# Two more up-projection chunks by seven products, four sums of down weights moved, and two copies put behind the norms, in a two-layer decoder trunk

## The chip, the cores and the metric

One core of one Trainium2 chip runs the whole program. The metric is the device time of one execution in microseconds (us); lower is better. The engines are named as in the profile: PE is TensorE (PEld its weight loads), DVE is VectorE, ACT is ScalarE, POOL is GpSimd and SP is SyncE, which here only issues DMAs.

## The reference, cut to what matters

```python
D_MODEL = 1024; SEQ = 512; DEPTH = 2; D_FF = 2816; CONV_W = 3

def conv_ffn(xn, w_up, cw, cb, w_down):
    a = xn @ w_up                                   # (512, 1024) x (1024, 5632)
    ap = jnp.pad(a, ((0, 0), (CONV_W - 1, 0), (0, 0)))
    a = sum(ap[:, j:j + T] * cw[j] for j in range(CONV_W)) + cb
    gate, val = jnp.split(a, 2, axis=-1)
    return (jax.nn.gelu(gate, approximate=True) * val) @ w_down

def reference(...):
    h = x
    for l in range(DEPTH):
        if l == 0: mix = dilated_mixer(rms_norm(h, g[0]), w_qkv_a[0], w_o_a[0], cos, sin)
        else:      # keys, values and forget gates are projected once from h
            kvf = rms_norm(h, kv_norm) @ w_kvf
            mix = fox_mixer(rms_norm(h, g[0]), w_q_b[0], w_o_b[0], k_sh, v_sh, c_sh)
        h = h + rms_norm(mix, g[1])
        h = h + rms_norm(conv_ffn(rms_norm(h, g[2]), w_up[l], conv_w[l], conv_b[l], w_down[l]), g[3])
    return h
```

All inputs are float32.

## The kernel before, in words

**Precision.** Each large product is made of three: an operand is split into a high part (a copy to the type fp32r, on ACT) and a low part (what is left, by a subtraction on DVE, or by a DMA that adds on the way, issued by POOL), and `mm3` adds high x high, high x low and low x high in PSUM. Its three lines are L292 to L294. In two forms `mm3` runs with a moving operand 512 wide or 256 wide.

**Weights.** `Weights` (`W`) hands out the weights in a fixed list of pieces of 128 x 1024. `load` issues the DMA on SP two pieces ahead, `high` makes the copy (L60) and `low` the subtraction (L69); `high_added` is a copy, a negated copy (L62) and the adding DMA (L86). `W.get()` returns the next piece and splits those up to `W.ahead` - 1 further, so the highs and lows of later pieces enter the queues of ACT and DVE at the place of that call. The order on each engine is the order in which the program is written.

**One layer.** Attention, output projection, up-projections in 22 chunks (a chunk is 128 columns of the gate and 128 of the value), down-projection. `h` stays on chip.

*The output projection* (`Proj.finish`) first takes two 128-row chunks of the weight through all four blocks of 128 positions, and then the last four chunks block by block, so that the blocks end one after the other. In the first layer a function `late` is called half-way through the first part. After each half block `Boundary.half` runs: mean square, multiply by the gain (`mix`, L337), the residual (L344), and, delayed by one block, the next norm (`norm`: square on ACT at L299, multiply on DVE at L309), and, delayed by two, `transpose`: eight PE transposes (L360), the split into `xh` and `xl` (L363, L364), and for blocks 0 and 1 two copies of the transposed values into `xlow` on ACT (L464); for blocks 2 and 3 two differences on DVE (L468, L469). `first_products` then begins chunks 0 and 1 with the first half of the positions, before blocks 2 and 3 are transposed.

*The up-projections* (`ffn`). A plain chunk multiplies two pieces with all 512 positions: 2 x 8 x 3 matmuls 512 wide. A chunk in `SEVEN` takes the product of 2 x 2 blocks by seven products of blocks instead of eight; each is 4 x 3 matmuls 256 wide:

```python
prod(o2, w.pop("S2"), (*XB, HI)); prod(o3, w.pop("S3"), (*XA, HI), True)
prod(o1, w.pop("A12"), x21);      prod(o2, w.pop("S1"), (*XA, LO))
prod(o3, w.pop("A22"), (*XB, LO));  opened = open_seven(m)   # A11 of the next chunk
prod(o2, w.pop("S4"), x22)
```

Between them stand three additions in PSUM on DVE (L1043, L1047, L1048) and copies on ACT (`u2` L1033, `s7` L1038, `s1` L1004). The weights of a seven-product chunk are made from two raw pieces in eight steps by the generator `seven_weights` (L732 to L764), advanced by `step` for the next chunk `m` and the one after, `n`. Each chunk's result passes the convolution taps (ACT L670, twice DVE L674), the GELU (L698), the product of gate and value on POOL (`product`, L693) and a DMA to `hD`. `post` does the taps and the GELU of a plain chunk one chunk later.

*The down-projection* works on pairs of 128-row chunks of the weight, 11 pairs, also by seven products. For it each pair needs four sums of weight blocks. `down_sums` makes these: three loads on SP, four subtractions on DVE (L639 to L642), and two stores of 512 KB to `dT`, from where `W` later loads them as pieces. It is a generator that its caller advances with `next`; `lag` and `behind` say how many calls later the subtractions and the stores follow the load. In this kernel the 22 pairs are summed so: ten of layer 0 and two of layer 1 beside the first projections, (0, 10) and (1, 8) in chunks 19 and 20 of layer 0, (1, 0) and (1, 1) beside the keys, four of layer 1 in the second attention, (1, 10) and (1, 9) in chunks 19 and 20 of layer 1. The activations of a pair are read back (`pair_load`), summed (`pair_sums`, L809 to L811), and their high and low parts are made by `pair_highs` (L819) and `pair_lows` (L824) for the first pairs while the last chunks still run.

**Memory.** Tiles come from pools of fixed slots: `t8` has 16 of 8 KB a partition, `t4` ten of 4 KB, `t2` eight of 2 KB, and PSUM has eight banks. An instruction that needs a slot waits until its last user is done.

Of the kernel before, what the change touches and what calls it, by code (L numbers as in the profile page):

```python
# [24 lines left out]
BIG = 3.0e38  # L25


SEVEN = tuple(range(3, 19))
ND = NF // 2
WARM = 6, 3  # L30
HALVES = [(slice(0, 1024),), (slice(0, 512), slice(512, 1024))]
# [77 lines left out]
def trunk_kernel(ctx, tc, x, norm_gains, w_qkv_a, w_o_a, w_q_b, w_o_b, kv_norm, w_kvf, b_f,  # L109
# [11 lines left out]
    def t8(shape, dt=F32, name="t8"):  # L121
        return p8.tile(shape, dt, tag="t8", name=name)
# [306 lines left out]
    class Boundary:  # L429
# [5 lines left out]

        def __init__(self, gain_mix, gain_next, name):
            self.mix, self.gain_next, self.name = Mix(gain_mix), gain_next, name
            self.xn, self.r = {}, {}
            self.xT = None

        def half(self, i, n, hf, o):
            b = self.order[i]
            self.mix.half(b, n, hf, o)
            if n == 0:
                if i >= 2:
                    self.transpose(self.order[i - 2])
                if i >= 1:
                    self.norm(self.order[i - 1])
            else:
                self.mix.add(b)  # L450

# [4 lines left out]
        def transpose(self, b):  # L456
            if self.xT is None:
                self.xT = new_xT(self.name)
                self.low = t8([128, 2, 4, 256], name="xlow")
            pts = transpose_in(b, self.xn.pop(b), self.xT)  # L460
            s = slice(b % 2 * 128, b % 2 * 128 + 128)
            if b < 2:
                for i, pt in enumerate(pts):
                    act.copy(self.low[:, i, :, s], pt)  # L464
# [127 lines left out]
    def first_products(bd, n):  # L592
        bd.norm(3)
        outs = [bank([128, T], name="first") for _ in range(n)]
        ws = []
        for i, o in enumerate(outs):
            ws.append(W.get())
            feat_mm(ws[i], bd.xT, o, LO)
            if i == 0:
                bd.transpose(2)  # L600
            if i == 2:
                bd.transpose(3)
        for w, o in zip(ws, outs):
            feat_mm(w, bd.xT, o, HI)
        return outs
# [58 lines left out]
    def ffn(l, bd, cp, nxt, ahead):  # L664
# [32 lines left out]
        def glu(c, bb):  # L697
            act.activation(bb[:, 0, :], bb[:, 0, :], AF.Gelu_apprx_tanh)  # L698
            gated.append((c, bb))

        def post(c, banks, between=None, bb=None):
            product()
            if bb is None:
                bb = taps(c, banks, between)
            else:
                first_tap(bb, 0, banks[0], c)
                other_taps(bb, 0, banks[0], c)
            glu(c, bb)

        xT = None  # L710
# [53 lines left out]
            dve.tensor_tensor(v[:, 1], r0, v[:, 0].bitcast(F32), ALU.subtract)  # L764

        def plain_weights(c):
            for _ in range(2):
                if c < NF - 2:
                    W.high_added()
                else:  # L770
                    W.high()
                    yield
                    W.low()
                if c < NF - 2:
                    yield

        gens = {}

# [6 lines left out]
            for _ in range(n):  # L785
                next(gens[c], None)

        def prepare(c, part):

            n = c + 2  # L790
            if n < NF and n not in SEVEN:
                step(n, 2 if part == 0 and n < NF - 2 else 1)
# [5 lines left out]
        def pair_load(j):  # L798

            if j < ND:  # L800
                acts[j] = k = t8([128, 1024], name="dact")
                sp.dma_start(k[:, 0:512], hD[2 * j])
                sp.dma_start(k[:, s2_], hD[2 * j + 1, :, 256:512])

# [184 lines left out]
        step(S0, 2)  # L989
        post(0, first[0:2])  # L990
        step(S0, 2)
        post(1, first[2:4])
        del first
        begun = opened = half_taps = None
        before = None

        def prod(o, w, x, start=False):
            half_mm(o, w, x[0:2], x[2], start)
# [8 lines left out]
        for c in range(2, NF):  # L1007
            if c == NF - 4:
                pair_load(0)
            if c == NF - 3:  # L1010
                sums = down_sums([(l, ND - 1), (1, 8 + l)], in_one, [pool], 1, 0)
                next(sums)
            m, n = c + 1, c + 2
            if c in SEVEN:
                x21, x22 = [(xT[0][i], xT[1][i], s) for i, s in ((1, LO), (1, HI))]
# [37 lines left out]
                if m in SEVEN:  # L1053
                    opened = open_seven(m)
                    step(m)
                else:
                    begun = W.get(), bank([128, T], name="up")
                    up(*begun, range(4))
                    step(n)
                other_taps(half_taps, 1, banks[1], NF + c)  # L1060
                prod(o2, w.pop("S4"), x22)
            else:
                banks = [bank([128, T], name="up") for _ in range(2)]
                for s in range(2):
                    if s == 0 and begun:
                        w, banks[0] = begun
                        up(*begun, range(4, KD))
                        begun = None
                    else:
                        up(W.get(), banks[s], range(KD))  # L1070
                    if c == NF - 2:
                        next(sums)
                    if s == 0 and before:
                        post(*before, (lambda: pair_lows(0)) if c == NF - 1 else None, half_taps)
                        half_taps = None
                        if c >= NF - 2:
                            pair_highs(c - NF + 2)
                            pair_sums(c - NF + 3)
                    if s == 0:
                        prepare(c, 0)  # L1080
                        if m in SEVEN:
                            opened = open_seven(m)
                    prepare(c, 1 + s)
                    if n in SEVEN:
                        step(n, 2)
            before = c, banks
            if c == NF - 3:
# [365 lines left out]
    combine(1, 1)  # L1453
    weigh(2, 1)

    rows = load_conv(0)
    grow = t2([16, 128], name="g_rows")
    sp.dma_start(grow[0:8, :], kv_norm.rearrange("(k p) -> k p", p=128))
# [4 lines left out]
    def late():  # L1463
        combine(2, 0)
        combine(2, 1)
        cp.append(conv_columns(rows))
        pg = bank([128, 16], name="g_ps")
        pe.transpose(pg, grow, ident[:16, :16])
        dve.tensor_copy(gcol, pg)

    bd = Boundary(load_gain(norm_gains[0, 1], "gain01"), load_gain(norm_gains[0, 2], "gain02"), "xb")
    Proj(6, 4, lambda kc: (OT[kc // 2][:, 0, kc % 2, :], OT[kc // 2][:, 1, kc % 2, :])).finish(bd, 4, late)


# [254 lines left out]
    for bp in range(2):  # L1729
# [5 lines left out]
        keep_values(1, 2 + bp, vb[bp])  # L1735
        keep_values(1, bp, vd[bp])
    del w22, S4
    W.ahead = 2
    W.split(W.n_split + 1)
    for bp in range(2):  # L1740
# [4 lines left out]
                mm3(vc[bp], ah, al, w4[s][0][:, k, :], w4[s][1][:, k, :], False, False, True)  # L1745
        keep_values(0, bp, vc[bp])
    del w4
    down1 = down_sums([(1, j) for j in range(2)], in_two, [pool, sp], 1, 1)
    for c in range(4, 8):
        if c == 7:  # L1750
            for i in range(4):
# [146 lines left out]
            W.split(W.n_get + 1)  # L1898
    f_bias(0, 0)
    f_bias(0, 1)  # L1900
    next(down1)
    M = len(pairs)
    sums, idle = {}, itertools.repeat(None)
    for j, m in ((2, 2), (3, 6), (4, 10), (5, 14)):
# [49 lines left out]
    W.ahead, W.ahead_dma = 4, 2  # L1954
    cp = conv_columns(load_conv(1))
    bd = Boundary(load_gain(norm_gains[1, 1], "gain11"), load_gain(norm_gains[1, 2], "gain12"), "xc")
    po.finish(bd, 4)


# [43 lines left out]
```

## Time and profile before

| | |
|---|---|
| median of 3 runs | 1101.36 us (1100.57 to 1102.66) |
| the profiled execution | 1100.13 us, its span 1098.4 us |
| PE busy | 1087.2 us |
| DVE busy | 890.8 us |
| ACT busy | 736.1 us |
| POOL busy | 304.4 us |
| first layer's output projection and its norm | about 141 to 187 us |
| first layer's chunks 2 to 21 | 202.4 to 409.2 us |
| keys | about 525 to 608 us |
| second layer's output projection and its norm | about 720 to 765 us |

A row of the trace in order of time gives the start, the duration, the engine, the line, the operation, what it writes and reads, its shape and, in brackets, how long the engine had stood before it and what ended that. `x2` at its end means two merged instructions. In a table of waits a row gives who waited for whom, the total, how often, and the longest.

### The profile page before, as it was taken

The page shows a single profiled execution, that of the slowest core. Times are in us where ns is not written, and L with a number is a line of the kernel's source. Part 1 is how long each engine was busy: PE and PEld are TensorE (multiplying, and loading weights), DVE is VectorE, ACT ScalarE, POOL GpSimd, SP SyncE. Part 2 cuts the span into 40 slices and gives each one's busy share as a digit, 9 for nine tenths or more (in the row PEclk, how much of TensorE's full clock was granted, in tenths as well). Part 3 has the DMA queues.
Part 4 walks back from the last instruction along what each step waited for, and adds up shares of the span by engine and source line. Part 5 has one row for each costly group of instructions (what it writes and reads, how often), then busy time and mean ns, then how long its engine had stood idle before and what let it go on. Part 6 is the DMA issues. An engine that isn't in the chain of part 4 may idle for free.

```text
span 1098.4 us, 19566 instructions
## 1 busy us (share of the span) xinstructions
PE 1087.2 (99%) x7040; PEld 960.8 (87%) x7040; DVE 890.8 (81%) x1468; ACT 736.1 (67%) x1264; POOL 304.4 (28%) x407
## 2 busy tenths in 40 slices
PE   9999999999999999999999999999999999999997
PEld 6988888999999988888888788788999999988886
DVE  5677767798888799897877878937798988799895
ACT  6644587688787547576565677766777878547473
POOL 4633010233333232000010677510233333232000
PEclk9999999999999999999999999999999999999999
DMA  9589894788888989794872777595688888989872
GB/s 320 132 282 408 333 222 118 153 216 206 211 210 205 270 305 341 277 325 97 211 154 77 219 225 199 167 287 134 145 208 209 219 208 207 251 316 336 301 249 77
DMA packets 191433, 247.90 MB, mean 226 GB/s; under 512 B 13472, under 2 KB 133272, under 8 KB 190824
## 3 DMA queue, kind: packets, MB, share of 16 engines
q1 hardware_dynamic: 168872, 177.67, 50.2%
q0 software_dynamic: 22464, 68.99, 27.4%
q8 instruction: 55, 0.90, 0.3%
q14 instruction: 42, 0.34, 0.1%
HBM read 170.28 MB, written 39.63 MB: 191 GB/s over the span
## 4 chain that ended last, share of the span: by engine, by line
PE 85%; ACT 6%; DVE 6%; issue 2%; DMA 0%; SPq 0%; DVEq 0%; ACTq 0%
PE up L292 11%; PE up L293 11%; PE up L294 11%; PE acc L292 7%; PE acc L293 7%; PE acc L294 7%; PE v_ps L292 2%; PE v_ps L293 2%; PE v_ps L294 2%; PE qk_ps L1336 2%; PE o_ps L1855 2%; PE s_ps L1808 2%; PE q_ps L292 2%; PE pT_ps L1840 2%; PE qk_ps L292 1%
## 5 line engine op out<-in xcount | busy, mean ns | idle before, releaser
L292 PE MATMUL up<-xsh,w 128*128 128x256 f32 x512 | 145.3, 284 | 1.0 <-ACT csum L1004 1.0
L293 PE MATMUL up<-xsl,w 128*128 128x256 f32 x512 | 144.9, 283 | 0.0
L294 PE MATMUL up<-xsh,w 128*128 128x256 f32 x512 | 144.9, 283 | 0.0
L674 DVE SCALAR_TENSOR_TENSOR bb<-up,conv,bb 128x511 f32<-128x511 f32 (+1 forms) x160 | 118.8, 747 | 18.1 <-ACT bb L670 15.2
L292 PE MATMUL acc<-w 128*128 128x512 f32 (+1 forms) x311 | 120.5, 388 | 0.0
L294 PE MATMUL acc<-w 128*128 128x512 f32 (+1 forms) x311 | 120.4, 387 | 0.0
L670 ACT ACTIVATE bb<-up,conv 128x512 f32<-128x512 f32 x80 | 62.1, 779 | 64.1 <-PE up L294 49.3
L293 PE MATMUL acc<-w 128*128 128x512 f32 (+1 forms) x267 | 103.2, 387 | 0.0
L292 PEld LDWEIGHTS up<-xsh,w 128*128 128x128 f32 x512 | 98.2, 192 | 1.7 <-ACT csum L1004 1.4
L293 PEld LDWEIGHTS up<-xsl,w 128*128 128x128 f32 x512 | 98.3, 192 | 0.1
L294 PEld LDWEIGHTS up<-xsh,w 128*128 128x128 f32 x512 | 98.3, 192 | 0.0
L60 ACT CAST w<-wraw 128x1024 fp32r<-128x1024 f32 x72 | 74.7, 1050 | 8.4 <-issue 3.8
L693 POOL TENSOR_TENSOR hc<-bb 128x512 f32<-128x512 f32 x44 | 69.0, 1567 | 38.1 <-ACT bb L698 38.0
L69 DVE TENSOR_TENSOR w<-wraw,w 128x1024 fp32r<-128x1024 f32 x50 | 61.3, 1240 | 14.4 <-ACT w L60 14.3
L294 PEld LDWEIGHTS acc<-w 128*128 128x128 f32 x311 | 58.4, 188 | 12.0
L292 PEld LDWEIGHTS acc<-w 128*128 128x128 f32 x311 | 58.4, 188 | 11.9
L741 POOL DMA_DIRECT2D w<-wraw x32 | 26.8, 839 | 143.7 <-ACT w L740 141.6
L292 PE MATMUL up<-xch,w 128*128 128x256 f32 (+1 forms) x192 | 61.5, 320 | 0.3
L292 PE MATMUL up<-xbh,w 128*128 128x256 f32 (+1 forms) x192 | 61.5, 320 | 0.3
L293 PE MATMUL up<-xcl,w 128*128 128x256 f32 (+1 forms) x192 | 61.1, 318 | 0.0
L293 PE MATMUL up<-xbl,w 128*128 128x256 f32 (+1 forms) x192 | 61.1, 318 | 0.0
L294 PE MATMUL up<-xch,w 128*128 128x256 f32 (+1 forms) x192 | 61.1, 318 | 0.0
(344 smaller groups left out, 3417.2 us busy)
## 6 DMA issues: line engine op xcount, KB each, us to landing
wraw<-in_w_up_dram SPq DMA_DIRECT2D x128, 256.0 KB, 3.2
w<-wraw POOLq DMA_DIRECT2D x54, 512.0 KB, 5.6
dT<-dsums SPq DMA_DIRECT2D x26, 512.0 KB, 4.0
wraw<-in_w_up_dram SPq DMA_DIRECT2D x24, 512.0 KB, 5.9
hD<-hc POOLq DMA_DIRECT2D x44, 256.0 KB, 4.3
dact<-hD SPq DMA_DIRECT2D x44, 256.0 KB, 6.1
wraw<-dT SPq DMA_DIRECT2D x22, 512.0 KB, 6.9
wraw<-in_w_down_dram SPq DMA_DIRECT2D x22, 512.0 KB
```

What stands on the lines that cost most here:

```text
L60: self.nc.scalar.copy(pair[:, 0, s], raw[:, s])
L69: self.nc.vector.tensor_tensor(pair[:, 1, s], raw[:, s], pair[:, 0, s].bitcast(F32), ALU.subtract)
L292: pe.matmul(o, ah, bh, start=first, stop=False, skip_group_check=shared)
L293: pe.matmul(o, ah, bl, start=False, stop=False, skip_group_check=shared)
L294: pe.matmul(o, al, bh, start=False, stop=last, skip_group_check=shared)
L670: act.activation(bb[:, i, :], ps, AF.Identity, bias=cp[:, 3, ch:ch + 1], scale=cp[:, 2, ch:ch + 1])
L674: dve.scalar_tensor_tensor(bb[:, i, n:], ps[:, :T - n], cp[:, 2 - n, ch:ch + 1], bb[:, i, n:], ALU.mult, ALU.add)
L693: pool.tensor_tensor(hc[c], bb[:, 0, :], bb[:, 1, :], ALU.mult)
L741: pool.dma_start(b[:, 1], r1, accum_op=ALU.add)
L1336: pe.matmul(o, ax(0, b, kc)[x], w[:, k, :], start=kc == 0 and x == 0 and w is wh, stop=kc == KD - 1 and w is wl)
L1808: pe.matmul(s[i][hh][:, :nn], q[a][rows, qs], k[b][rows, :nn], start=n == 0, stop=n == 2)
L1840: pe.transpose(o[:, k0 + k, :], p[:, hh, k * 128:(k + 1) * 128], ident)
```

## The change

Two chunks fewer stay plain: `SEVEN` takes in chunks 19 and 20, so of the chunks after 2 only 21 is plain. The sums of the four pairs that were made in chunks 19 and 20 are made elsewhere: (0, 10) and (1, 8) in the first output projection, (1, 9) beside the keys ahead of (1, 0) and (1, 1), and (1, 10) in the second output projection. In `Boundary` the copies into `xlow` become a function of their own, `keep`, which is called after the next block's norm. The taps of chunk 1 are written after the first half of chunk 2. The activations of the first two pairs come from `t4` instead of `t8`.

```diff
-SEVEN = tuple(range(3, 19))
+SEVEN = tuple(range(3, 21))
...
         def half(self, i, n, hf, o):                      # Boundary
             if n == 0:
                 if i >= 2: self.transpose(self.order[i - 2])
                 if i >= 1: self.norm(self.order[i - 1])
+                if i >= 2:
+                    self.keep(self.order[i - 2])
+                next(self.beside, None)
...
-            pts = transpose_in(b, self.xn.pop(b), self.xT)
-            s = slice(b % 2 * 128, b % 2 * 128 + 128)
+            self.pts[b] = transpose_in(b, self.xn.pop(b), self.xT)
+
+        def keep(self, b):
+            pts, s = self.pts.pop(b), slice(b % 2 * 128, b % 2 * 128 + 128)
             if b < 2:
                 for i, pt in enumerate(pts):
                     act.copy(self.low[:, i, :, s], pt)
...
         def post(c, banks, between=None, bb=None):        # in the branch with bb given
                 other_taps(bb, 0, banks[0], c)
+                if between is not None:
+                    between()
...
-                acts[j] = k = t8([128, 1024], name="dact")
+                acts[j] = k = (t8 if j > 1 else t4)([128, 1024], name="dact")
...
-        post(1, first[2:4])
-        before = None
+        before = 1, first[2:4]
...
-            if c == NF - 3:
-                sums = down_sums([(l, ND - 1), (1, 8 + l)], in_one, [pool], 1, 0)
-                next(sums)
...
                     begun = W.get(), bank([128, T], name="up")      # after the last seven-product chunk
                     up(*begun, range(4))
-                    step(n)
+                    XA.clear()
+                    XB.clear()
+                    step(m)
+                    pair_highs(0)
+                    pair_sums(1)
...
-                    if c == NF - 2:
-                        next(sums)
-                    if s == 0 and before:
+                    if s == 0 and m in SEVEN:
+                        opened = open_seven(m)
+                        step(n, 2)
+                    if s == 0:
                         post(*before, (lambda: pair_lows(0)) if c == NF - 1 else None, half_taps)
...
+    beside = down_sums([(0, ND - 1), (1, 8)], in_one, [sp], 2, 2)    # first output projection
+    next(beside)
+    next(beside)
     rows = load_conv(0)
...
         dve.tensor_copy(gcol, pg)                                    # the end of late()
+        next(beside)
+        next(beside)
...
+    bd.beside = beside
...
+    down1 = down_sums([(1, j) for j in (9, 0, 1)], in_two, [pool, pool, sp], 1, 1)   # values and keys
+    next(down1)
     W.ahead = 2
...
     del w4
-    down1 = down_sums([(1, j) for j in range(2)], in_two, [pool, sp], 1, 1)
+    next(down1)
...
     f_bias(0, 1)
-    next(down1)
...
+    bd.beside = down_sums([(1, ND - 1)], in_one, [sp], 1, 1)          # second output projection
+    next(bd.beside)
     po.finish(bd, 4)
```

More of the change, by code (lines that the diff above doesn't have):

```diff
@@ L437, in __init__ @@
             self.mix, self.gain_next, self.name = Mix(gain_mix), gain_next, name
-            self.xn, self.r = {}, {}
-            self.xT = None
+            self.xn, self.r, self.pts = {}, {}, {}
+            self.xT, self.beside = None, iter(())
         def half(self, i, n, hf, o):
@@ L600, in first_products @@
                 bd.transpose(2)
+                bd.keep(2)
             if i == 2:
                 bd.transpose(3)
+                bd.keep(3)
         for w, o in zip(ws, outs):
@@ L766, in plain_weights @@
         def plain_weights(c):
[L767 to L775, printed above, removed]
+            W.high_added()
+            yield
+            W.high()
+            yield
+            W.low()
         gens = {}
@@ L786, in step @@
                 next(gens[c], None)
[L788 to L792, printed above, removed]
         acts, one, two, raws, later2 = {}, {}, {}, {}, {}
@@ L991, in ffn @@
         step(S0, 2)
-        post(1, first[2:4])
-        del first
         begun = opened = half_taps = None
-        before = None
+        before = 1, first[2:4]
         def prod(o, w, x, start=False):
@@ L1078, in ffn @@
                             pair_sums(c - NF + 3)
[L1079 to L1084, printed above, removed]
+                    if n not in SEVEN:
+                        step(n, 2 - s)
+                    elif s == 1:
                         step(n, 2)
```

## The prediction, made before the changed kernel was run

> **What bounds the kernel.** I read the page's busy shares and chain first, then the waits of the tensor engine (PE), then its rows in order of time, then the rows of the vector engine (DVE) and the scalar engine (ACT) at each place that the change touches.
>
> ```profile
> span 1098.4 us, 19566 instructions
> PE 1087.2 (99%) x7040; PEld 960.8 (87%) x7040; DVE 890.8 (81%) x1468; ACT 736.1 (67%) x1264; POOL 304.4 (28%) x407
> ...
> PE 85%; ACT 6%; DVE 6%; issue 2%; DMA 0%; SPq 0%; DVEq 0%; ACTq 0%
> ...
> L670 ACT ACTIVATE bb<-up,conv 128x512 f32<-128x512 f32 x80 | 62.1, 779 | 64.1 <-PE up L294 49.3
> ```
>
> PE is busy for 99% and the chain runs through it. So a gain comes only from less PE work or from a PE wait taken away, and a loss only from a new PE wait. The waits are few:
>
> ```profile
> PE xt_ps L360 <- DVE xn L309: 1.1, 2, 0.5
> PE up L292 <- ACT csum L1004: 1.0, 2, 0.5
> ```
>
> Busy time of overlapping matmuls hides short stalls, so I price PE by start-to-start times. First and last of 119 matmuls 256 wide, then first and last of 13 matmuls 512 wide:
>
> ```profile
> 188.08 0.28 PE L293 MATMUL first<-xbl,w 128*128 128x256 f32 x1
> ...
> 202.24 0.28 PE L294 MATMUL first<-xbh,w 128*128 128x256 f32 x1
> ...
> 409.18 0.39 PE L292 MATMUL acc<-w 128*128 128x512 f32 x1
> ...
> 411.90 0.39 PE L292 MATMUL acc<-w 128*128 128x512 f32 x1
> ```
>
> That is 14.16/118 = 0.120 us and 2.72/12 = 0.227 us.
>
> **The change, part by part.** *Chunks 19 and 20 by seven products.* A plain chunk is 2 x 8 x 3 = 48 matmuls, 10.9 us; by seven it is 7 x 4 x 3 = 84 of half width, 10.1 us. The saving is 0.82 us a chunk, for four chunks **-3.3 us**. [...]
>
> *Copies behind the norms.* At each output projection PE stands for the last transposes:
>
> ```profile
> 757.69 0.28 PE L294 MATMUL first<-xch,w 128*128 128x256 f32 x1
> 758.49 1.29 PE L360 MATMUL xt_ps<-ident,xn 128*128 128x128 f32 x8 [0.53 <-DVE xn L309]
> 759.54 0.36 PE L292 MATMUL first<-xch,w 128*128 128x256 f32 x1
> ...
> 187.09 1.03 PE L360 MATMUL xt_ps<-ident,xn 128*128 128x128 f32 x8
> 187.88 0.36 PE L292 MATMUL first<-xbh,w 128*128 128x256 f32 x1
> ...
> 176.51 1.19 ACT L464 COPY xlow<-xt_ps 128x512 f32<-128x512 f32 x2 [1.65 <-DVE xbl L364]
> 177.59 1.06 ACT L299 ACTIVATE junk<-h 128x1024 bf16<-128x1024 f32 x1
> ```
>
> The start is 0.80 - 0.12 = 0.68 us late, and the eight transposes take 1.05 us against 0.79 us elsewhere: 0.95 us. The two copies (1.19 us) stand in ACT's queue ahead of the square that begins the next norm, once for each of blocks 0 and 1. Behind it they cost nothing on this chain, and the chain is over 1.2 us earlier: the wait goes, in both layers **-1.9 us**. What is late next is the multiply of the output projection's last half on DVE, which no matmul waits for within 3 us.
>
> *Sums of four pairs.* Four DVE subtractions make one pair; first of four and the next operation:
>
> ```profile
> 387.01 0.68 DVE L639 TENSOR_TENSOR dsums<-dsums 128x512 f32<-128x512 f32 x1
> ...
> 389.79 2.96 DVE L674 SCALAR_TENSOR_TENSOR bb<-up,conv,bb 128x511 f32<-128x511 f32 x4
> ```
>
> So 2.78 us a pair. Each also issues three loads on SP and two stores. In the first output projection the sums of two pairs stand in `late`, behind the copy of gcol:
>
> ```profile
> 150.09 0.16 DVE L1469 COPY gcol<-g_ps 128x16 f32<-128x16 f32 x1
> 150.17 1.21 DVE L69 TENSOR_TENSOR w<-wraw,w 128x1024 fp32r<-128x1024 f32 x1
> 156.76 0.15 DVE L334 TENSOR_SCALAR vr<-ss 128x1 f32<-128x1 f32 x1 [5.39 <-ACT junk L330]
> ...
> 155.33 0.39 PE L293 MATMUL acc<-w,OT 128*128 128x512 f32 x1
> ```
>
> DVE has 5.39 us free there and the sums need 5.56, but what is queued behind them is the low part of the last output weight (the row at 150.17): `W.get` for it is called after `late`. It would end at 150.17 + 5.56 + 1.21 = 156.94. By the order of the loop (24 matmuls, then 3 x 3, then the first of that weight) the matmul at 155.33 is the first to read it: **+1.6 us**. Bounds: 0 if the low part is elsewhere in the order, 2.8 if the sums also wait for their loads. Those six loads go ahead of the conv rows and the last output weight on SP; ACT's use of that weight moves by at most their issue time, which the 1.6 covers. In the second output projection the one pair's sums follow the first multiply of block 0:
>
> ```profile
> 737.78 0.69 DVE L337 TENSOR_TENSOR mix<-acc,gain 128x512 f32<-128x512 f32 x1 [1.45 <-ACT junk L330]
> 739.38 0.17 DVE L342 RECIPROCAL rs<-sd 128x1 f32<-128x1 f32 x1 [0.92 <-ACT sd L332]
> ```
>
> They fill 1.45 us of idle time and push this multiply to about 739.0; the reciprocal behind it waits for ACT until 739.38 anyway, and moves 0.3 us. The shorter norm chain covers that: 0 (bounds 0 and 0.3).
>
> The stores stand on SP behind all loads of the projection, and the next up loads behind them are asked for only after it.
>
> In the keys three pairs are summed where two were. The pair behind the value products falls into idle DVE time (first row). The next now stands behind keys(6), ahead of the low part for keys(7):
>
> ```profile
> 582.93 1.23 DVE L69 TENSOR_TENSOR w<-wraw,w 128x1024 fp32r<-128x1024 f32 x1 [2.52 <-ACT w L60]
> ...
> 600.45 1.21 DVE L69 TENSOR_TENSOR w<-wraw,w 128x1024 fp32r<-128x1024 f32 x1
> 601.58 1.21 DVE L1564 TENSOR_TENSOR_SCAN c<-one,zz 16x512 f32<-16x512 f32 x1
> ...
> 606.71 1.22 DVE L69 TENSOR_TENSOR w<-wraw,w 128x1024 fp32r<-128x1024 f32 x1
> ...
> 603.15 0.39 PE L293 MATMUL k_ps<-xkl,w 128*128 128x512 f32 x1
> ```
>
> That low part would end at 600.45 + 2.78 + 1.21 = 604.4, and PE reads it at 603.15: 1.3 us; the next one (606.71) moves alike and costs some 0.2 more. **+1.5 us**, bounds 0 (if the order differs) and 2.8. Behind the store of the last pair on SP stands the load of ck, and behind that the first bias:
>
> ```profile
> 611.29 1.15 POOL L1789 TENSOR_SCALAR bias<-ck,cq 128x128 f32<-128x128 f32 x2 [4.43 <-DMA ck<-cd]
> ...
> 616.54 0.48 DVE L1828 TENSOR_SCALAR bias<-bias,rl 128x128 f32<-128x128 f32 x2
> ...
> 619.92 0.38 PE L1840 MATMUL pT_ps<-ident,bias 128*128 128x128 f32 x2
> ```
>
> The bias comes some 3.8 us later (an estimate: 2.78 of the third pair's sums, which the store waits for, and 1 of its issue), PE itself is 1.5 later, and the normalised row was ready 2.9 us before its transpose: covered, 0 (up to 1). The stores that POOL now issues here stand ahead of nothing but the store of c, and are due 15 us before it.
>
> *What the two new seven-product chunks do to DVE and ACT.* In a steady chunk DVE waits for PE only once for long:
>
> ```profile
> 353.06 0.43 DVE L1043 TENSOR_TENSOR up<-up,csum 128x256 f32<-128x256 f32 x1 [0.83 <-PE up L294]
> ...
> 403.65 0.42 DVE L809 TENSOR_TENSOR dact<-dact 128x256 f32<-128x256 f32 x1
> ...
> 404.91 1.53 DVE L674 SCALAR_TENSOR_TENSOR bb<-up,conv,bb 128x511 f32<-128x511 f32 x2
> 406.35 1.91 DVE L824 TENSOR_TENSOR w<-dact,w 128x1024 fp32r<-128x1024 f32 x1
> 408.18 2.35 DVE L824 TENSOR_TENSOR w<-wraw,w 128x1024 fp32r<-128x1024 f32 x2
> 410.45 1.52 DVE L674 SCALAR_TENSOR_TENSOR bb<-up,conv,bb 128x511 f32<-128x511 f32 x2
> ...
> 405.87 1.30 POOL L693 TENSOR_TENSOR hc<-bb 128x512 f32<-128x512 f32 x1
> ```
>
> Chunk 20's gate half is now ready only with its seventh product. Then 36 matmuls of chunk 21 and 12 of the first down pair follow, and the second matmul behind them reads the low part of pair 1: 49 x 0.227 = 11.1 us. DVE's queue in that time: ACT's first tap (0.78, and 0.2 to start), two taps 1.44, three low parts of pair 0 at 1.135, the three sums of pair 2 (1.26), two taps 1.44, then two low parts of pair 1, the first of 1.14 to 1.91 (1.91 when it meets POOL's product, as at 406.35) and 1.14: 10.8 to 11.6 us. The third is needed 0.68 us after the second and comes 1.14 after it. I take **+0.5 us a layer, +1.0**; bounds 0, and 1.9 a layer if pair 0's low parts meet POOL too and the products' weights land late. The sums of two pairs (5.6 us of DVE, six loads on SP, four stores on POOL ahead of its products) leave chunks 19 and 20, which is what makes room. The extra ACT work ahead of u2 in chunk 17 moves to chunk 19: 0.
>
> *Post of chunk 1 moved into chunk 2, and the first two activations in the smaller pool.* The same instructions in another order on ACT; hidden by the 48 matmuls of chunk 2. Taken as 0; bounds -1.0 and +1.0, the waits on csum (1.0 in the waits) vanishing or doubling.
>
> **Sum.** -3.3 - 1.9 + 1.6 + 1.5 + 1.0 = -1.1 us. The profiled execution took 1100.13 us (1098.4 of it span), 1.2 below the median of 1101.36; it would become 1099.0, and the median 1100.3.
>
> **The rivals.** *The moved sums stay hidden.* If all three new waits are absent, -5.2 us: 1096.2. For it: DVE is idle for 19% of the span, and no wait of PE for a low part is in the list today, though other pairs are summed beside projections. Against: engines run their queues in order, and both low parts have under 5.6 and 2.8 us to spare. *DVE bounds the end of the up-projections (slower).* Place: from chunk 20's seventh product to the second down pair. Without the 1.0 the sum is -2.1; each microsecond of wait there counts twice, so it is slower by 2.2 us from 2.2 us a layer. At 2.9 (0.5, two more meetings with POOL of 0.7 each, weights 1.0 late): 1101.4 - 2.1 + 5.8 = 1105.1. For it: the DVE rows from 403.65 to 410.45 follow each other without a gap. Against: 5.6 us leave that stretch. *The copies do not do what they are moved for*, since xcl on DVE holds the chain: the 1.9 is lost, 1102.2. Against: DVE had long been idle at that norm. [...]
>
> **How the numbers follow.** Forecast 0.51 (own range 1098.5 to 1102.5), sums hidden 0.26, DVE bounds 0.15, copies idle 0.06, the rule 0.02. About 0.2%, 2.2 us, is what a measurement of this kernel can tell. Faster by more takes the second case, the rule and a little of the first: 0.30; slower 0.15; within 0.55. Range 1096.0 to 1104.0.
>
> **What would show it.** After: 168 more matmuls 256 wide and 96 fewer 512 wide in each layer; no wait of xt_ps for xn; new PE waits of acc for a low part (L69) near 155 us, of k_ps for one near 603 us, and of acc for L824 where the down-projection begins, in both layers. The prediction is wrong if the first two of these are missing, or if the third is over 2 us.

## The result and the profile after

| | before | after |
|---|---|---|
| median | 1101.21 us of 4 runs (1100.57 to 1102.66) | 1108.12 us of 4 runs (1107.48 to 1110.14) |
| the profiled execution | 1100.13 us, span 1098.4 | 1108.61 us, span 1106.8 |
| PE busy | 1087.2 us | 1086.2 us |
| DVE busy | 890.8 us | 902.4 us |

The ratio is 1.0064, with a 95% interval of 1.0047 to 1.0081: the changed kernel is slower by 0.6%, where the prediction said no measurable change (1100.3, range to 1104.0). First the head of the page of the changed kernel:

```profile
span 1106.8 us, 19977 instructions
...
PE 1086.2 (98%) x7184; PEld 964.4 (87%) x7184; DVE 902.4 (82%) x1494; ACT 751.1 (68%) x1290; POOL 303.5 (27%) x407
```

PE does less work than before in a longer span, so the loss is waiting. The table of PE's waits (total, how often, the longest):

```profile
PE o_ps L1860 <- ACT pT L1847: 2.7, 2, 2.1
PE acc L293 <- DVE w L824: 1.8, 4, 0.8
PE xt_ps L360 <- DVE xn L309: 1.6, 1, 1.6
PE acc L293 <- DVE w L69: 1.5, 1, 1.5
PE q_ps L294 <- DMA w<-wraw: 1.3, 1, 1.3
...
PE k_ps L294 <- DVE w L69: 1.0, 1, 1.0
```

Three of the six were predicted: acc for L824, acc for L69 and k_ps for L69. The wait of xt_ps for xn looks like the old one that was to vanish, but it is another: it stands once, at the first transposes of the second output projection, and the old ones at the last transposes are gone. The waits of o_ps and q_ps lie in the second attention, of which the change only takes out one call, the `next(down1)` behind `f_bias(0, 1)`.

**The ledger.** The table gives, for one and the same matmul in both traces, how much later it starts after the change, and what each stretch between two such marks added.

| stretch | later at its end (us) | added | predicted |
|---|---|---|---|
| load of x (start) | +0.75 | +0.75 | 0 |
| first output projection, low part of its last weight | +2.40 | +1.65 | +1.6 |
| last transposes, layer 0 | +1.57 | -0.83 | -0.95 |
| chunks 2 to 21, layer 0 | -0.05 | -1.62 | -1.64 |
| start of the down-projection, layer 0 | +1.33 | +1.38 | +0.5 |
| keys | +2.59 | +1.26 | +1.5 |
| second attention | +7.40 | **+4.81** | **0** |
| first transposes, second output projection | +9.43 | **+2.03** | **0** |
| last transposes, layer 1 | +8.48 | -0.95 | -0.95 |
| chunks 2 to 21, layer 1 | +6.85 | -1.63 | -1.64 |
| start of the down-projection, layer 1 | +8.22 | +1.37 | +0.5 |

The load of x is not part of the change: the matmul that waits for it starts at 7.85 us in this execution, at 7.10 before, and between 6.87 and 7.79 in the nine variants of the changed kernel below, which leave that part alone. Without it the ledger gives +7.5, against +6.9 between the medians. The two rows in bold hold 6.8 of it.

**The second attention.** In order of time, DVE, then PE, POOL and SP of the changed kernel:

```profile
601.91 0.68 DVE L647 TENSOR_TENSOR dsums<-dsums 128x512 f32<-128x512 f32 x1
...
604.69 1.22 DVE L69 TENSOR_TENSOR w<-wraw,w 128x1024 fp32r<-128x1024 f32 x1
605.83 1.21 DVE L1567 TENSOR_TENSOR_SCAN c<-one,zz 16x512 f32<-16x512 f32 x1
```

```profile
605.96 0.50 PE L294 MATMUL k_ps<-xkh,w 128*128 128x512 f32 x1 [0.97 <-DVE w L69]
```

```profile
607.77 0.52 POOL L1569 DMA_DIRECT2D cd<-c  x1 [22.25 <-DVE c L1568]
...
618.37 0.73 POOL L1794 TENSOR_SCALAR bias<-ck,cq 128x128 f32<-128x128 f32 x2 [9.00 <-DMA ck<-cd]
```

```profile
608.83 1.79 SPq L655 DMA_DIRECT2D dT<-dsums  x2
610.73 2.50 SPq L1588 DMA_DIRECT2D ck<-cd  x2
```

The four subtractions from 601.91 stand ahead of the low part (the predicted wait of k_ps) and also ahead of the scan that makes c. SP's queue and POOL's of the kernel before, for the same place:

```profile
605.46 0.33 SPq L1585 DMA_DIRECT2D ck<-cd  x1
611.36 0.33 SPq L647 DMA_DIRECT2D dT<-dsums  x1
```

```profile
603.54 0.56 POOL L1566 DMA_DIRECT2D cd<-c  x1 [39.83 <-DVE c L1565]
```

So the store of c is issued 4.23 us later (607.77 against 603.54), the load of ck 5.27 us later (610.73 against 605.46) and now behind the last stores, and it takes 7.64 us to the first bias (618.37) where it took 5.83: the first bias is 4.23 + 1.04 + 1.81 = 7.08 us late, and PE only 2.6. PE then stands:

```profile
628.38 1.14 PE L1860 MATMUL o_ps<-pT,Vt 128*64 128x128 f32 x12 [2.09 <-ACT pT L1847]
```

```profile
633.51 0.50 PE L294 MATMUL q_ps<-xqh,w 128*128 128x512 f32 x1 [1.28 <-DMA w<-wraw]
```

The second wait has another cause besides. The low part of a query weight is a DMA that POOL issues between the biases, here after the change and before it:

```profile
625.33 0.91 POOL L86 DMA_DIRECT2D w<-wraw  x1 [0.79 <-ACT w L62]
```

```profile
619.95 0.90 POOL L86 DMA_DIRECT2D w<-wraw  x1 [0.79 <-ACT w L62]
```

It goes out 5.38 us later, but PE is 5.36 us late itself by then, behind the first wait. What makes PE stand is that this DMA takes 8.14 us to land where it took 5.67. It is back to 6.12 and 5.21 us in the first two experiments, where the first wait is gone and this one too; what lengthens it here is not shown.

**The second output projection.** ACT, DVE and PE of the changed kernel:

```profile
732.54 1.05 ACT L60 CAST w<-wraw 128x1024 fp32r<-128x1024 f32 x1 [3.51 <-DMA wraw<-in_w_o_b_dram]
...
745.32 0.58 ACT L330 ACTIVATE junk<-acc 128x512 bf16<-128x512 f32 x1
```

```profile
746.71 0.68 DVE L647 TENSOR_TENSOR dsums<-dsums 128x512 f32<-128x512 f32 x1
...
749.49 0.68 DVE L337 TENSOR_TENSOR mix<-acc,gain 128x512 f32<-128x512 f32 x1
...
753.30 1.42 DVE L309 SCALAR_TENSOR_TENSOR xn<-h,rs,gain 128x512 f32<-128x512 f32 x2
```

```profile
754.11 1.10 PE L360 MATMUL xt_ps<-ident,xn 128*128 128x128 f32 x6 [1.59 <-DVE xn L309]
```

The kernel before had the first mean square here:

```profile
734.86 0.57 ACT L330 ACTIVATE junk<-acc 128x512 bf16<-128x512 f32 x1
```

ACT waits for raw weights, longest for the second of the output weights (3.51 us in the row shown; the longest such wait before was 2.11), because the pair's three loads stand on SP ahead of them, and begins the first mean square at 745.32. With PE 7.40 later than before that is 3.06 us too late. In the eighth experiment below, which has neither these loads nor these subtractions in this place, it begins at 734.77, after 0.90 us of waiting for PE. The subtractions then push the second multiply, which the prediction's row had at 737.78, to 749.49.

**The start of the down-projection.** ACT, DVE and PE:

```profile
400.59 1.05 ACT L819 CAST w<-dact 128x1024 fp32r<-128x1024 f32 x1
401.54 0.78 ACT L678 ACTIVATE bb<-up,conv 128x512 f32<-128x512 f32 x1
```

```profile
402.36 1.53 DVE L682 SCALAR_TENSOR_TENSOR bb<-up,conv,bb 128x511 f32<-128x511 f32 x2 [0.61 <-ACT bb L678]
...
409.91 1.90 DVE L824 TENSOR_TENSOR w<-dact,w 128x1024 fp32r<-128x1024 f32 x1
411.74 2.35 DVE L824 TENSOR_TENSOR w<-wraw,w 128x1024 fp32r<-128x1024 f32 x2
```

```profile
413.00 0.50 PE L293 MATMUL acc<-w 128*128 128x512 f32 x1 [0.76 <-DVE w L824]
...
414.14 0.50 PE L293 MATMUL acc<-w 128*128 128x512 f32 x1 [0.17 <-DVE w L824]
```

The matmul at 413.00 is the second of the second pair; it reads the second low part, the one at 414.14 the third.

### The profile page after: what moved, and what is told of

It is laid out like the page before. It is cut to its first block, busy times and chain, and to the rows that moved or that the text cites. A ratio compares the mean times of both kernels' runs of the same rounds, so it can differ in the third digit from the quotient of the medians.

```text
span 1106.8 us, 19977 instructions
## 1 busy us (share of the span) xinstructions
PE 1086.2 (98%) x7184; PEld 964.4 (87%) x7184; DVE 902.4 (82%) x1494; ACT 751.1 (68%) x1290; POOL 303.5 (27%) x407
## 5 line engine op out<-in xcount | busy, mean ns | idle before, releaser
L292 PE MATMUL up<-xsh,w 128*128 128x256 f32 x576 | 163.2, 283 | 1.0 <-ACT csum L1002 1.0
L293 PE MATMUL up<-xsl,w 128*128 128x256 f32 x576 | 163.0, 283 | 0.0
L294 PE MATMUL up<-xsh,w 128*128 128x256 f32 x576 | 163.0, 283 | 0.0
L682 DVE SCALAR_TENSOR_TENSOR bb<-up,conv,bb 128x511 f32<-128x511 f32 (+1 forms) x160 | 119.3, 748 | 14.5 <-ACT bb L678 11.6
L292 PEld LDWEIGHTS up<-xsh,w 128*128 128x128 f32 x576 | 110.6, 192 | 1.4 <-ACT csum L1002 1.4
L293 PEld LDWEIGHTS up<-xsl,w 128*128 128x128 f32 x576 | 110.6, 192 | 0.1
L294 PEld LDWEIGHTS up<-xsh,w 128*128 128x128 f32 x576 | 110.6, 192 | 0.0
L60 ACT CAST w<-wraw 128x1024 fp32r<-128x1024 f32 x64 | 66.8, 1053 | 12.4 <-DMA wraw<-in_w_o_b_dram 4.2
L292 PEld LDWEIGHTS acc<-w 128*128 128x128 f32 x311 | 58.4, 188 | 12.0
L294 PEld LDWEIGHTS acc<-w 128*128 128x128 f32 x311 | 58.4, 188 | 11.8
L69 DVE TENSOR_TENSOR w<-wraw,w 128x1024 fp32r<-128x1024 f32 x44 | 54.3, 1243 | 10.7 <-ACT w L60 8.8
L762 ACT CAST w<-wsum 128x1024 fp32r<-128x1024 f32 x36 | 38.0, 1054 | 36.8 <-DVE wsum L759 36.8
L293 PEld LDWEIGHTS acc<-w 128*128 128x128 f32 x267 | 50.1, 188 | 13.5 <-DVE w L824 3.6
L292 PE MATMUL up<-xbh,w 128*128 128x256 f32 (+1 forms) x176 | 53.6, 304 | 0.5 <-ACT csum L1028 0.3
L292 PE MATMUL up<-xch,w 128*128 128x256 f32 (+1 forms) x176 | 53.5, 304 | 0.5 <-DVE up L1042 0.2
L824 DVE TENSOR_TENSOR w<-wraw,w 128x1024 fp32r<-128x1024 f32 x44 | 54.0, 1268 | 0.0
```

The costliest lines, as they stand in the source:

```text
L60: self.nc.scalar.copy(pair[:, 0, s], raw[:, s])
L69: self.nc.vector.tensor_tensor(pair[:, 1, s], raw[:, s], pair[:, 0, s].bitcast(F32), ALU.subtract)
L292: pe.matmul(o, ah, bh, start=first, stop=False, skip_group_check=shared)
L293: pe.matmul(o, ah, bl, start=False, stop=False, skip_group_check=shared)
L294: pe.matmul(o, al, bh, start=False, stop=last, skip_group_check=shared)
L682: dve.scalar_tensor_tensor(bb[:, i, n:], ps[:, :T - n], cp[:, 2 - n, ch:ch + 1], bb[:, i, n:], ALU.mult, ALU.add)
```

## The experiments

The theory: the change's parts do what they were costed to do, and the loss lies in queues at three places: ck behind c and behind the last stores, the sums and loads in the second output projection, and DVE's order at the start of the down-projection. The rival: three pairs are simply too much beside the keys, and the two new chunks cost more than they save.

**1. The pair (1, 9) alone in spare time, (1, 0) and (1, 1) in their old places.**

```diff
-    down1 = down_sums([(1, j) for j in (9, 0, 1)], in_two, [pool, pool, sp], 1, 1)
-    next(down1)
+    down9 = down_sums([(1, 9)], in_two, [pool], 1, 1)
+    next(down9)
...
     del w4
-    next(down1)
+    next(down9)
+    down1 = down_sums([(1, j) for j in range(2)], in_two, [pool, sp], 1, 1)
...
         if c == 6:
+            next(down9)
             next(down1)
...
     f_bias(0, 1)
+    next(down1)
```

> The changed kernel with only the order beside the keys altered: the pair (1, 9) keeps its place behind the value products, and the pairs (1, 0) and (1, 1) get back their places of the kernel before (behind the scan that makes c, the last pair's sums between the keys and the first bias, its stores behind the first biases). Theory A (queue order): the low part for keys(7) and c stood behind four subtractions, and the load of ck behind the last stores; with the old order the wait of k_ps for that low part (1.1 us in the changed kernel) and the 4.8 us lost between keys(7) and the end of the second attention both go: 1108.1 - 6.1 = about 1102. Rival B (load): three pairs beside the keys cost DVE and DMA time wherever they stand, so at least the 4.8 stay: about 1107.

1101.40 us (before 1100.72 on the same chip; ratio 1.0008, interval 0.9999 to 1.0017). POOL and SP:

```profile
604.62 0.51 POOL L1569 DMA_DIRECT2D cd<-c  x1 [19.51 <-DVE c L1568]
...
612.32 1.14 POOL L1796 TENSOR_SCALAR bias<-ck,cq 128x128 f32<-128x128 f32 x2 [4.38 <-DMA ck<-cd]
```

The first bias comes 6.05 us earlier, the waits of k_ps, o_ps (2.1) and q_ps are gone, and 6.7 us come back (6.2 if each kernel is taken against the kernel before as measured beside it). 1.4 of it is the wait of xt_ps in the second output projection, which shrinks from 1.6 to 0.2 us and which neither theory had counted. Theory A holds: the third pair costs nothing where nothing waits behind it.

**2. Only the last stores moved behind the first biases.**

```diff
-    next(down1)
     load_ck(0)
...
     f_bias(0, 1)
+    next(down1)
```

> The changed kernel with one call moved: the last stores beside the keys (SP) are issued behind the first two biases instead of ahead of the load of ck. The four subtractions ahead of the low part and of c stay, so the k_ps wait (1.1 us) stays. Theory A (the stores ahead of ck): the first bias on POOL, 7.1 us later than before the change (618.4 against 611.3), comes some 3 us earlier (the issue of ck 1 us, its flight 7.6 back to 5.8 us), and most of the 4.8 us after keys(7) goes: about 1104. Theory B (c itself is late, 4.2 us behind the subtractions): ck cannot be issued more than 1 us earlier, and under 1.5 us come back: about 1107.

1102.92 us (before 1100.72; ratio 1.0021, interval 1.0011 to 1.0030): 5.2 us from one call (4.7 against the kernel before as measured beside each). SP and POOL:

```profile
609.26 0.34 SPq L1588 DMA_DIRECT2D ck<-cd  x1
609.70 0.87 SPq L655 DMA_DIRECT2D dT<-dsums  x2
```

```profile
607.37 0.52 POOL L1569 DMA_DIRECT2D cd<-c  x1 [22.22 <-DVE c L1568]
...
614.37 0.72 POOL L1793 TENSOR_SCALAR bias<-ck,cq 128x128 f32<-128x128 f32 x2 [5.41 <-DMA ck<-cd]
```

c is as late as in the changed kernel; ck is issued 1.5 us earlier and takes 5.11 us to the first bias instead of 7.64, with the last megabyte of stores behind it and not ahead. The bias is 4.0 us earlier, and all of the 4.8 us in the attention is back. The wait of k_ps (1.0) stays, as expected. So the order of two calls on SP was the largest single loss. That c is late does not reach PE by itself: here it is as late as after the change and the bias 3.08 us later than before the change, and PE does not wait for it.

**3. The sums of the first output projection behind the low part.**

```diff
     dve.tensor_copy(gcol, pg)
-    next(beside)
-    next(beside)
...
                     self.step(n + i, b, hf)
+                    if hook is not None and (b, hf, i) == (0, 0, 0):
+                        next(bd.beside)
+                        next(bd.beside)
```

> The changed kernel with the subtractions of (0, 10) and (1, 8) in the first output projection put behind the low part of the last output weight instead of ahead of it. By the prediction's step the wait of acc for that low part (1.65 us at 157.7) goes and the first multiply of the projection comes some 0.5 us later at most: 1106.5. Rival: the low part was late because its raw weight came late behind the six loads on SP, or the mean square now waits instead: under 0.5 us comes back, 1107.8.

1106.47 us (before 1100.72; ratio 1.0053, interval 1.0035 to 1.0071), 1.65 less than the changed kernel. DVE and PE:

```profile
150.38 1.27 DVE L69 TENSOR_TENSOR w<-wraw,w 128x1024 fp32r<-128x1024 f32 x1
...
156.53 0.69 DVE L653 TENSOR_TENSOR dsums<-dsums 128x512 f32<-128x512 f32 x1
```

```profile
155.62 0.39 PE L293 MATMUL acc<-w,OT 128*128 128x512 f32 x1
```

The matmul starts without a wait and the same eight subtractions, 5.6 us, are hidden; their six loads still stand on SP ahead of the raw weight, so the rival's late raw weight is out. This rests on the trace: the four runs lie between 1104.28 and 1108.55 us, so that their median agrees with the 1.65 is in part luck.

**4. No subtractions in the second output projection.**

```diff
-    def down_sums(pairs, place, queue, lag, behind):
+    def down_sums(pairs, place, queue, lag, behind, subtract=True):
...
-            if 0 <= i - lag < n:
+            if 0 <= i - lag < n and subtract:
...
-    bd.beside = down_sums([(1, ND - 1)], in_one, [sp], 1, 1)
+    bd.beside = down_sums([(1, ND - 1)], in_one, [sp], 1, 1, False)
```

> The changed kernel without the four subtractions of the pair (1, 10) in the second output projection; its three loads and two stores stay (what is stored are the unsummed blocks, so the last pair's weights are not the right ones). The first transposes there wait 1.75 us for xn, and xn is 3.3 us later against PE than before the change. Theory A (the subtractions on DVE, 2.8 us ahead of the second multiply): xn comes 1.9 us earlier and the wait goes: 1106.3. Theory B (the loads: ACT's copies of the up weights stand up to 0.8 us each for their raw weights, so the first mean square is 3 us late): the wait stays at over 1 us: 1107.8.

1106.01 us (before 1100.72; ratio 1.0050, interval 1.0035 to 1.0065). The wait is gone:

```profile
751.36 0.82 PE L360 MATMUL xt_ps<-ident,xn 128*128 128x128 f32 x6
```

Theory A by its result, but not alone. In the first experiment, with the subtractions in place, this wait had already shrunk to 0.2 us, since ACT's first mean square was only 1.7 us too late there (737.49, with PE 0.97 later than before the change). So the wait needs both: late raw weights alone cost PE nothing here (the mean square at 743.30, with PE 6.40 later, is 2.04 us too late), with the subtractions it is 0.2 us when the mean square is 1.7 us late and 1.6 us when it is 3.06 late. The subtractions with weights in time were not run in this place.

**5. The low parts of the second down pair ahead of chunk 21's taps.**

```diff
-        post(*before, lambda: pair_lows(1))
+        pair_lows(1)
+        post(*before)
```

> The changed kernel with the low parts of the second down pair put ahead of all taps of chunk 21 on DVE (they stood between its two halves). In the changed kernel PE waits for the second and third of these low parts, 0.92 and 0.33 us a layer, where the kernel before had no such wait. Theory A (the order in DVE's queue): the low parts end 1.5 us earlier, in time for PE, and 1.25 to 1.37 us a layer come back: 1108.1 - 2.6 = 1105.5. Rival B (what is late is the copy on ACT of the last of the three high parts, or the taps, now 3.4 us later, hold a PSUM bank that the down-projection waits for): under 1 us comes back, 1107.5 or more.

1109.10 us (before 1100.74; ratio 1.0078, interval 1.0063 to 1.0093): nothing gained. By the same matmuls in the two traces PE wins 1.04 us at the second pair and loses 1.38 at the third. ACT and PE:

```profile
414.51 0.63 ACT L706 ACTIVATE bb<-bb 128x512 f32<-128x512 f32 x1 [4.46 <-DVE bb L682]
415.05 1.99 ACT L819 CAST w<-wraw 128x1024 fp32r<-128x1024 f32 x2
```

```profile
421.56 0.50 PE L293 MATMUL acc<-w 128*128 128x512 f32 x1 [0.76 <-DVE w L824]
```

The taps now end later, the GELU (L706) waits for them on ACT, and the third pair's high parts (L819) stand behind the GELU. The number is in the rival's range, but neither theory had named this: the wait moved one pair on, through ACT's queue.

**6. The up-projection code of the kernel before, with the sums in their new places.** The body of `ffn` is that of the kernel before, without its two `next(sums)` and the `down_sums` they advance, and `SEVEN = tuple(range(3, 19))`.

> The changed kernel with the up-projection code of the kernel before (chunks 3 to 18 by seven, 19 and 20 plain, taps of chunk 1 ahead of chunk 2), without the sums that stood there; the sums stay in their new places and the copies stay behind the norms. Theory A (the ledger of the two traces: 0.81 us saved a chunk, four chunks, against 1.37 us of wait for low parts a layer): +3.25 - 2.74 = +0.5 us, 1108.6. Theory B (the transition is not made slow by the two chunks but by something else, and the chunks are worth their 3.3 us): 1111.4. Theory C (the two chunks cost more elsewhere than their place shows): under 1107.

1108.75 us (before 1100.74; ratio 1.0081, interval 1.0064 to 1.0098), 0.6 more than the changed kernel, as theory A had it. The interval reaches from 1107.8 to 1111.5 us, so the time rules out theory C but not theory B; the traces decide. By the same matmuls in both traces the chunks cost 1.64 us a layer more and the start of the down-projection 1.37 less. As the change was built, its four seven-product chunks are worth about 0.5 us.

**7. The kernel before with only the copies moved.** `transpose` and `keep` as in the change; all else as before.

> The kernel before with nothing changed but the copies into the low half, put behind the next block's norm. By the prediction 0.95 us a layer come out of PE's waits for the last transposes: 1100.7 - 1.9 = 1098.8; by the ledger of the two traces 0.83 + 0.95: 1098.9. Rival: the chain of the last norm gains, but the seven-product chunks wait for the lower half's sums instead: 1100.7.

1099.00 us (before 1100.74; ratio 0.9984, interval 0.9975 to 0.9993): 1.74 us less, and nothing later takes it back.

**8. Four pairs beside the keys, none in the second output projection.** As the first experiment, and:

```diff
-    down9 = down_sums([(1, 9)], in_two, [pool], 1, 1)
+    down9 = down_sums([(1, 9), (1, 10)], in_two, [pool], 1, 1)
...
+        if c == 4:
+            W.split(W.n_get + W.ahead)
+            next(down9)
         keys(c)
...
-    bd.beside = down_sums([(1, ND - 1)], in_one, [sp], 1, 1)
-    next(bd.beside)
```

> The changed kernel with all four layer-1 pairs beside the keys and none in the second output projection: (1, 9) and (1, 10) where DVE stands idle (2.5 and 3.3 us, behind the value products and in keys(4)), (1, 0) and (1, 1) in the places of the kernel before. Theory A (a pair costs nothing where DVE is idle and nothing waits behind it): 6.7 us as in the run with (1, 9) alone, and the 2.1 us of the second output projection: 1099.3. Rival B (the fourth pair's load waits on SP for a slot and holds the query weights behind it, or its 1 MB meets the other loads): a wait of q_ps or k_ps for a raw weight appears and the 2.1 are lost again: 1101.4 or more.

1099.29 us (before 1100.74; ratio 0.9987, interval 0.9978 to 0.9997), as theory A had it. DVE beside keys(4):

```profile
583.76 1.22 DVE L69 TENSOR_TENSOR w<-wraw,w 128x1024 fp32r<-128x1024 f32 x1
584.89 0.68 DVE L647 TENSOR_TENSOR dsums<-dsums 128x512 f32<-128x512 f32 x1
...
588.03 0.69 DVE L1532 TENSOR_TENSOR kst<-k_ps,kst 128x512 fp32r<-128x512 f32 x1 [0.28 <-ACT kst L1531]
```

The second spare pair fills the stretch in which DVE waited 3.1 us for kst, and leaves 0.28 of it.

**9 and 10. The parts together.** The eighth with the third experiment's edit; then also the low parts of pair 1 and the high parts of pair 2 ahead of chunk 21's taps and GELU:

```diff
-        post(*before, lambda: pair_lows(1))
-        pair_highs(2)
+        pair_lows(1)
+        pair_highs(2)
+        post(*before)
         pair_sums(3)
```

> The changed kernel with four pairs beside the keys (as in the run with four pairs there) and with the sums of the first output projection behind the low part. If the losses are separate waits, they add: 1099.3 - 1.65 = 1097.6, below the kernel before by 3.1 us. If one wait covers for another (the time won at 157 us is lost at the next wait for a weight), 1099.3.

> The same, and at the down-projection the low parts of pair 1 and the high parts of pair 2 ahead of the taps and the GELU of chunk 21. With the low parts alone moved, PE waited for the low parts of pair 2 instead (1.3 us a layer), because ACT's copies of its high parts stood behind the GELU, which stood behind the taps. Theory A (only that order held them): both waits go, 2.5 us more than the run without this: 1095.1. Rival B (DVE simply has more to do between chunk 20's seventh product and pair 2 than PE gives it time for: 11.8 us of work for pairs 0 and 1 and 5 us more for taps and sums): the wait moves on to another low part, and less than 1 us is gained: 1097.0 or more.

Before was 1101.04 us here. The first took 1098.23 (ratio 0.9974, interval 0.9964 to 0.9984), 1.06 less than the eighth where 1.65 was expected if the losses add. Each against the kernel before as measured beside it, it is 1.36 less, and in the two profiled executions the same matmul at 156.90 us starts 1.60 us earlier and the last ones 1.69: the losses add. The second took 1096.58 (ratio 0.9961, interval 0.9948 to 0.9973), 1.65 less again where theory A had 2.5. Of its waits there stays:

```profile
PE acc L293 <- DVE w L827: 0.7, 4, 0.2
```

So the wait for low parts fell from 1.8 to 0.7 us, and the rival's limit is what remains: DVE works without a wait from 400.01 us, at chunk 20's last taps, until past the second of these waits, at 419.41. This version is faster than the kernel before by 0.4% and than the changed one by about 1%.

## Why the prediction was wrong

Five of its terms came out within 0.3 us. The sum was wrong by two places that it had set to zero and one that it had set too small. Of its signs the matmul counts came (x7184 against x7040) and so did the three new waits, none of them over 2 us. A wait of xt_ps for xn was to be absent: the old two are, but a new one stands at another place. No sign was put at the second attention, where most of the loss lay.

- *Chunks by seven, -3.3:* measured -3.25, with the trace's own start-to-start times. Right. (48 x 0.2267 - 84 x 0.120 is 0.80 a chunk, not 0.82; it changes nothing.) The 0.02 that the chances give to "the rule" stood for a larger saving here, which no run shows.
- *Copies behind norms, -1.9:* measured -1.8 in the ledger and -1.74 alone. Right, and for the reason given.
- *Sums in the first output projection, +1.6:* measured +1.65, and the wait is gone in the third experiment with the subtractions behind the low part. Right.
- *Low part in the keys, +1.5:* measured +1.26. Right.
- *"covered, 0 (up to 1)" for ck: the step that failed.* It put the first bias 3.8 us late and held it covered by PE's own 1.5 and 2.9 us of room. The bias was 7.08 us late. The step counted one pair's subtractions and an issue. It left out that c itself stands behind the subtractions ahead of the low part, although it had just moved that low part by them: the scan is the next row in its own quoted list, at 601.58. And it left out that the stores also lengthen the flight of ck, 7.64 us against 5.83. With 7.1 in place of 3.8 its own rule gives 7.1 - 4.4 = 2.7 us of wait, or 1.6 with PE 2.6 us late as it was and not 1.5, and PE waited 2.09 for o_ps. The query weight's DMA, which no term had, added 1.45 of the 4.81, smaller waits the rest. Of the two omissions the second decided: with the stores moved behind the bias (the second experiment) c was as late, and the whole 4.8 us came back.
- *"0 (bounds 0 and 0.3)" in the second output projection: failed too.* It priced the subtractions against idle DVE time at their old place in time, and of the DMAs only the stores. The pair's three loads stand ahead of the last output weights and the up weights on SP, and ACT's queue waits for those with the first mean square behind them. So the mean square was 3.06 us late before the subtractions began. In the first output projection it had counted the loads of the moved sums on SP, where they cost nothing (the third experiment keeps them and has no wait); here it did not. Measured: 2.03 us.
- *The start of the down-projection, +0.5 a layer, bounds 0 and 1.9:* measured +1.37. The mechanism and the place were right, the term too small. ACT's first tap waited for the three high copies of pair 0 (the rows to 401.54), where 0.2 us to start had been assumed; DVE's taps began at 402.36, 1.4 us after chunk 20's seventh product (36 matmuls of 0.227 us ahead of the first acc at 409.14, so 400.97), not 0.98, and the first low part took the upper value, 1.90 (409.91 to 411.81, beside POOL's product from 409.42 to 410.72; the low part at 403.81, with no product beside it, took 1.22). By its own figures the upper value would have been 0.5 us for the second low part (11.6 against 11.1) and 0.46 more for the third; the 0.41 of the late taps makes it 1.37. The upper part of the bounds was the slower rival, which had named the right place but needed 2.2 us a layer to decide the sign; at 1.37 it did not.
- *Post of chunk 1 and the smaller pool, 0:* no matmul of those chunks shifts against its neighbours by 0.25 us. Right.

## What to carry to other kernels

When work is put into an engine's queue ahead of something, the rows behind it have to be followed to their last reader through every queue: here four subtractions delayed not only a low part but a scan, a store, a load and the first bias, and the place of two stores on another queue decided whether PE felt it. Idle time on an engine can be filled for nothing if the next instruction in its queue was itself waiting (in the eighth experiment four subtractions took 3.1 us of waiting down to 0.28); the place to put work is directly behind the last urgent instruction before such a wait, and the same three pairs beside the keys cost over 6 us or nearly nothing by their place and that of their stores. A moved step should be costed with its DMAs against the loads that it overtakes.

## What the runs showed of the hardware

In three of the profiled executions a wait of PE cost more than its length. In that of the third experiment the granted clock falls to half (0.50) behind a wait of 1.74 us. Rows of the table by stretches (the column before the last two is the granted clock), then PE in order of time:

```profile
752.00:753.00 1.00, 1.00 (x9) 0.72 (x7) 0.96 (x4) 0.67 (x3) 0.00 (x0) 0.99 0.92 302
753.00:754.00 1.00, 1.00 (x4) 0.81 (x3) 1.00 (x1) 0.55 (x1) 0.00 (x0) 0.50 1.01 402
...
756.00:757.00 1.00, 1.00 (x5) 0.82 (x4) 0.96 (x4) 0.68 (x2) 0.00 (x0) 0.81 0.13 53
```

```profile
751.60 1.32 PE L360 MATMUL xt_ps<-ident,xn 128*128 128x128 f32 x8 [1.74 <-DVE xn L309]
...
753.43 0.63 PE L294 MATMUL acc<-w,OTb 128*128 128x512 f32 x1
753.85 0.63 PE L292 MATMUL acc<-w,OTb 128*128 128x512 f32 x1
```

The start-to-start time is 0.42 us there instead of 0.227. The wait of 2.09 us for o_ps stands in five profiled executions (the changed kernel's, and those of experiments 3 to 6); behind it the clock was halved in three of them, those of experiments 3 to 5, and not in the changed kernel's own nor in the sixth experiment's. The four halved stretches last 3.4 us three times and 6.8 us once. None was found before the last matmul of the seven executions whose longest wait was 1.5 us or less (the kernel before, experiments 1, 2 and 7 to 10). Why a wait of 2.09 us is followed by a halved stretch in three executions and not in two is not shown.
